# Conditioning product with w_cond as the moving operand, in two float32r parts

## The chip, the cores and the metric

The kernel runs on one core of a Trainium2 chip. The metric is the device time of one execution in microseconds (us). A core has five engines with a queue each: PE (matmul; its weight loads are shown apart as PEld), DVE (vector), ACT (scalar), POOL and SP. In this kernel SP issues most DMA transfers and POOL some.

## The reference

One layer of a decoder trunk on 2048 prompt rows and 64 sample rows (8 sequences of 8) of width 1024. Ahead of everything stands a conditioning by a vector c (one for the prompt, eight for the samples, so nine rows):

```python
def _layer(x, c, ...):
    mod = jax.nn.silu(c) @ w_cond + b_cond            # (9, 1024) @ (1024, 3072)
    shift, scale, gate = jnp.split(mod, 3, axis=-1)
    h = _rmsnorm(x, g_pre) * (1 + scale[:, None, :]) + shift[:, None, :]
    proj = h @ w_in                                    # (.., 1024) @ (1024, 10240)
    ...                                                # gMLP branch, dilated attention branch, merge
    out = merged @ w_out
    x_new = x + gate[:, None, :] * _rmsnorm(out, g_post)
```

The change touches the product for shift and scale alone, that is silu(c) times the first 2048 columns of w_cond, all in float32.

## The kernel before

The program is one stream of work without outer repetition. `conditioning` computes from c the two tables that everything else needs: `A` (1 + scale, times g_pre) and `Sh` (shift), each as 128 partitions x 8 blocks of 128 channels x 9 rows. Then the x tiles (16 of 128 prompt rows, one of 64 sample rows) are transposed on PE (L630), scaled and shifted by A and Sh (DVE L640, ACT L642) and split into two float16 parts hH and hL. From these the value projections of the first pattern are made (`v_tile`, L652 and after), and then, over some 2400 us, the query, key, value, gate and branch products, the attention, and the output projections.

A scheduler orders the instructions of each engine from the dependences and priorities; conditioning, the first units of w_in and the first x tile have high priority. Each queue runs in the order that the scheduler left. A tile from a pool with a number of buffers (`bufs`) waits, when the buffers are used up, until the readers of the oldest one are done.

Inside `conditioning`, in the order of the code:

- c9 (nine rows of c) is loaded, then w_cond in four chunks `wc` of 512 columns each (two loads of 1 MB per chunk, three buffers). Between the chunks the generator `loads_between` issues the load of x tile 0 (`x_tiles`, which also squares the tile on ACT, L712, takes the root, L167, and scales the tile, L715) and the first six loads of w_in (`wr`, L294).
- silu(c) is made from tanh (L202, L204, L205), transposed by eight small PE products (L208) and copied to `sc9`; scT holds it as two float32r parts (columns 0 to 8 the high part, 32 to 40 the rest), for later use in `gate_rows`.
- `vec` brings the small vectors, transposed at L214 into vecT.
- The product, L219 to L225: 16 blocks of 128 columns of w_cond, for each eight products with a 128x128 block of w_cond as the standing operand (the weights that PE loads first) and the nine columns of sc9 as the moving one. All 16 results stand in one PSUM bank, as columns of channels.
- L228 to L230 turn them into Sh and A. L232 to L248 find a scale `bm` over both and apply it.

Beside that, ACT takes absolute maxima of the w_in loads (L310, `junk`), from which their float16 scale comes.

`cond_mm` is a helper that `gate_rows` uses much later for the third part of w_cond: it splits a 128x512 tile into a high part wcH (ACT copy to float32r) and the rest wcL (DVE subtraction), and multiplies both with scT as the standing operand, so that rows 0 to 8 of the PSUM result belong to the high part of silu(c) and rows 32 to 40 to its rest.

Of the kernel before, what the change touches and what calls it, by code (L numbers as in the profile page):

```python
# [10 lines left out]
F32 = mybir.dt.float32  # L11
# [3 lines left out]
AF = mybir.ActivationFunctionType  # L15
ALU = mybir.AluOpType
AX = mybir.AxisListType

D = 1024
SEQ = 2048  # L20
KC = D // 128
# [48 lines left out]
def body(ctx, tc, I, O):  # L70
    nc = tc.nc
    PE, DMA = nc.tensor, nc.sync.dma_start

    V, S = nc.vector, nc.scalar
# [21 lines left out]
    CHB = 2  # L96
    WRB = 6
    HLB = 8
    BANKS = {"mm": 3, "s0": 1, "s1": 1, "o": 1, "t": 2}
    turn = [0]  # L100
    CXB = 3
# [5 lines left out]
    def bank(tag, shape=(128, 512), bufs=None, dt=F32):  # L107
        if tag == "s":
            turn[0] += 1
            tag = ("s0", "s1")[turn[0] % 2]  # L110
        return ps.tile(list(shape), dt, tag=tag, bufs=BANKS[tag], name=tag)

# [6 lines left out]
    ident = const.tile([128, 128], F32, name="ident")  # L119
# [30 lines left out]
    A = const.tile([128, KC, 9], F32, name="A")  # L150
# [10 lines left out]
    w_cond = I["w_cond"][0]  # L161
# [23 lines left out]
    def conditioning(cp, loads_between):  # L185
        c9 = cp.tile([9, D], F32, name="c9")
        DMA(c9[0:1], I["c_prompt"])
        DMA(c9[1:9], I["c_sample"])
        vec = cp.tile([40, 128], F32, name="vec")
        GDMA(vec[0:8], I["g_pre"].rearrange("o (k p) -> (o k) p", p=128))  # L190
        GDMA(vec[8:16], I["ln_v_g"].rearrange("o (k p) -> (o k) p", p=128))
        GDMA(vec[16:24], I["ln_v_b"].rearrange("o (k p) -> (o k) p", p=128))
        GDMA(vec[24:40], I["b_cond"][:, 0:2 * D].rearrange("o (k p) -> (o k) p", p=128))
        chunks = []
        for q in range(4):
            w = cp.tile([128, KC, 512], F32, tag="wc", bufs=3, name="wc")
            for k in (0, 4):
                DMA(w[:, k:k + 4], w_cond[k * 128:(k + 4) * 128, q * 512:(q + 1) * 512].rearrange("(k p) c -> p k c", p=128))
            chunks.append(w)
            loads_between(q)  # L200
        th = cp.tile([128, D], F32, tag="sq", bufs=1, name="th")[0:9]
        S.activation(th, c9, AF.Tanh, scale=0.5)  # L202
        V.memset(scT.bitcast(F32), 0.0)
        V.scalar_tensor_tensor(c9, th, 1.0, c9, op0=ALU.add, op1=ALU.mult)  # L204
        V.tensor_scalar(c9, c9, 0.5, None, op0=ALU.mult)  # L205
        pt = bank("t")
        for kc in range(KC):
            PE.transpose(pt[:, kc * 9:kc * 9 + 9], c9[:, kc * 128:(kc + 1) * 128], ident[0:9, 0:9])  # L208
        sc9 = cp.tile([128, KC, 9], F32, name="sc9")
        V.tensor_copy(sc9, pt[:, 0:72].rearrange("p (k n) -> p k n", n=9))  # L210
        S.activation(scT[:, :, 0:9], sc9, AF.Copy)
        V.tensor_tensor(scT[:, :, 32:41], sc9, scT[:, :, 0:9], op=ALU.subtract)
        pv = bank("t")
        PE.transpose(pv[:, 0:40], vec, ident[0:40, 0:40])  # L214
        vecT = cp.tile([128, 5, KC], F32, name="vecT")
        V.tensor_copy(vecT, pv[:, 0:40].rearrange("p (a k) -> p a k", a=5))
        V.tensor_copy(lngb, vecT[:, 1:3])

        pm = bank("o")  # L219
        for q in range(4):  # L220
            for j in range(4):
                o = (q * 4 + j) * 9
                for kc in range(KC):
                    PE.matmul(pm[:, o:o + 9], chunks[q][:, kc, j * 128:(j + 1) * 128], sc9[:, kc, :],  # L224
                              start=kc == 0, stop=kc == KC - 1)  # L225
        p4 = pm[:, 0:144].rearrange("p (a k n) -> p a k n", a=2, n=9)
        v4 = vecT.unsqueeze(3).to_broadcast([128, 5, KC, 9])
        V.tensor_tensor(Sh, p4[:, 0], v4[:, 3], op=ALU.add)  # L228
        V.scalar_tensor_tensor(A, p4[:, 1], 1.0, v4[:, 4], op0=ALU.add, op1=ALU.add)
        V.tensor_tensor(A, A, v4[:, 0], op=ALU.mult)  # L230

        bm = cp.tile([128, 2], F32, name="bm")  # L232
        for i, x in enumerate((A, Sh)):
            V.tensor_reduce(bm[:, i:i + 1], x.rearrange("p k n -> p (k n)"), axis=AX.X, op=ALU.max,
                            apply_absolute_value=True)
        V.tensor_tensor(bm[:, 0:1], bm[:, 0:1], bm[:, 1:2], op=ALU.add)
        pt = bank("t")
        PE.transpose(pt[0:1, 0:128], bm[:, 0:1], ident)
        b1 = cp.tile([1, 1], F32, name="b1")
        V.tensor_reduce(b1, pt[0:1, 0:128], axis=AX.X, op=ALU.max)  # L240
        pt = bank("t")
        PE.matmul(pt[:, 0:1], onesk[0:1, :], b1, start=True, stop=True)
        V.tensor_scalar(bm[:, 0:1], pt[:, 0:1], 32.0, 1e-30, op0=ALU.mult, op1=ALU.max)
        V.reciprocal(bm[:, 1:2], bm[:, 0:1])
        for x in (A, Sh):
            V.tensor_scalar(x, x, bm[:, 1:2], None, op0=ALU.mult)
        for i, f in enumerate((1.0, 0.5, -0.125)):
            V.tensor_scalar(hsc[:, i:i + 1], bm[:, 0:1], f, None, op0=ALU.mult)  # L248
# [454 lines left out]
    with tc.tile_pool(name="prep", bufs=1) as pp:  # L703
        loaded = {}

        def x_tiles():
            for i, (t0, n) in enumerate(tiles):
                xt = pp.tile([128, D], F32, tag="x", bufs=6, name="x")
                DMA(xt[0:n], x_src(i)[0])
                sq = pp.tile([128, D], F32, tag="sq", bufs=1, name="sq")  # L710
                r = rst[0:n, i:i + 1]
                S.activation(sq[0:n], xt[0:n], AF.Square, accum_out=r)  # L712
                rsqrt(r, n)
                eng = V if i % 2 or i == 0 else nc.gpsimd
                eng.tensor_scalar(xt[0:n], xt[0:n], r, None, op0=ALU.mult)  # L715
                loaded[i] = (t0, n, xt)
                yield

        xg = x_tiles()

        def loads_between(q):
            if q == 1:
                next(xg)
            if q == 2:
                next(loading)

        with tc.high_priority():
            conditioning(pp, loads_between)
            v0 = [load_unit16(OVV)]
            modulate(pp, [loaded[0]])  # L730
        v0.append(load_unit16(OVV + 512))
        DMA(masks, I["c_masks"])
        for batch in ((0,), (1,), (2, 3), (4, 5, 6, 7), (8, 9, 10, 11), (12, 13, 14, 15), (16,)):
            while batch[-1] not in loaded:
                next(xg)
            if batch[0]:
                modulate(pp, [loaded[i] for i in batch])
            for i in batch:
                for g in range(2):
                    v_tile(g, 0, *v0[g], *tiles[i])  # L740
                next(splitting)
# [592 lines left out]
```

## Time and profile before

| | |
|---|---|
| median of three runs | 2623.76 us (2620.62 to 2625.17) |
| profiled execution, its own time | 2629.5 us |
| its span, first to last instruction | 2627.7 us |
| busy: PE, PEld, DVE, ACT, POOL | 2509.3, 1817.9, 1589.1, 1110.8, 340.4 us |
| moved by DMA | 384.22 MB, mean 146 GB/s |

All lines of the profile are of one execution. Starts are us from the begin of the span. A line of a group gives the code line, the engine, the operation, output<-input by the program's tile names, count, busy time and mean ns of one; behind the bar what the engine waited for ahead of it. A line of a list of one tile gives the least, median and largest duration in ns. PE's matmul records overlap, so the distance between starts, not the duration, is what one costs in a stream.

### The profile page before, as it was taken

What the parts mean: (1) busy time and instruction counts of PE and PEld (TensorE: products, weight loads), DVE (VectorE), ACT (ScalarE), POOL (GpSimd) and SP (SyncE); (2) the same over time, 40 slices, a digit from 0 to 9 for tenths busy, and PEclk for the clock granted to TensorE, in tenths of its full rate; (3) what the DMA queues carried; (4) which work ended last, traced back from release to release, by engine and by line L of the source; (5) the groups of instructions that cost most, each with busy time, mean ns of one, the idle gap of its engine ahead of it and who ended that gap; (6) DMA issues with size and microseconds to landing.
All of it is one profiled execution on the core that took longest, in us unless ns stands there. A gap on an engine that the chain in (4) does not pass through costs nothing.

```text
span 2627.7 us, 48620 instructions
## 1 busy us (share of the span) xinstructions
PE 2509.3 (95%) x18678; PEld 1817.9 (69%) x18678; DVE 1589.1 (60%) x3590; ACT 1110.8 (42%) x2759; POOL 340.4 (13%) x459
## 2 busy tenths in 40 slices
PE   6899999999999989999989988999999999999998
PEld 6785768767677555555555677856556568898998
DVE  1663445878967789687877666854323235555553
ACT  2544556545545554544445423332323224343422
POOL 1020000120121211212012210001000001111110
PEclk9999999999999999999999999999999999999999
DMA  5323555576874777866687764352212057657552
GB/s 204 108 86 75 134 127 132 120 178 156 196 191 119 160 175 186 180 141 173 154 195 171 184 171 143 118 166 70 77 58 66 21 181 228 194 170 220 180 166 73
DMA packets 529863, 384.22 MB, mean 146 GB/s; under 512 B 184959, under 2 KB 472847, under 8 KB 529630
## 3 DMA queue, kind: packets, MB, share of 16 engines
q1 hardware_dynamic: 505022, 315.48, 44.7%
q0 software_dynamic: 24608, 65.63, 9.6%
q8 instruction: 146, 2.39, 0.4%
q14 instruction: 87, 0.71, 0.1%
HBM read 250.85 MB, written 90.78 MB: 130 GB/s over the span
## 4 chain that ended last, share of the span: by engine, by line
PE 69%; DMA 13%; DVE 9%; issue 6%; ACT 2%; SPq 1%; POOL 1%; DVEq 0%; ACTq 0%; POOLq 0%
PE mm L373 13%; PE mm L374 13%; PE mm L375 13%; PE mm L383 5%; PE mm L384 5%; PE mm L385 5%; DMA ch<-in_cache_kv_w 3%; PE o L224 2%; DMA wg<-in_w_cond 1%; PE s L892 1%; PE o L941 1%; DMA raw<-ya 1%; PE s L1153 1%; PE s L383 1%; DVE S L503 1%
## 5 line engine op out<-in xcount | busy, mean ns | idle before, releaser
L373 PE MATMUL mm<-hH,hl 128*128 128x512 f16 (+2 forms) x2240 | 770.7, 344 | 0.0
L374 PE MATMUL mm<-hL,hl 128*128 128x512 f16 (+2 forms) x2240 | 769.9, 344 | 0.0
L375 PE MATMUL mm<-hH,hl 128*128 128x512 f16 (+2 forms) x2240 | 769.6, 344 | 0.0
L383 PE MATMUL mm<-hl,hH 128*128 128x256 f16 x1536 | 418.4, 275 | 5.0 <-ACT zb L680 3.1
L384 PE MATMUL mm<-hl,hL 128*128 128x256 f16 x1536 | 420.7, 275 | 0.1
L385 PE MATMUL mm<-hl,hH 128*128 128x256 f16 x1536 | 420.3, 275 | 0.5 <-DVE hl L326 0.5
L373 PEld LDWEIGHTS <-hl 128*128 128x128 f16 x2240 | 223.3, 100 | 184.3 <-issue 10.1
L375 PEld LDWEIGHTS <-hl 128*128 128x128 f16 x2240 | 220.8, 99 | 181.4 <-issue 1.1
L374 PEld LDWEIGHTS <-hl 128*128 128x128 f16 x2240 | 220.6, 98 | 171.3 <-issue 0.6
L902 ACT ACTIVATE p<-p,sg 128x256 f32<-128x256 f32 (+1 forms) x384 | 172.4, 450 | 138.9 <-DVE sg L900 122.2
L430 POOL DMA_DIRECT2D ch<-in_cache_kv_w x104 | 93.2, 897 | 681.5 <-DVE pr L564 213.9
L383 PEld LDWEIGHTS <-hH 128*128 128x128 f16 x1536 | 152.3, 99 | 25.9 <-issue 4.8
L384 PEld LDWEIGHTS <-hL 128*128 128x128 f16 x1536 | 151.6, 99 | 25.2 <-issue 5.9
L385 PEld LDWEIGHTS <-hH 128*128 128x128 f16 x1536 | 151.8, 99 | 19.6 <-issue 1.2
L279 POOL TENSOR_TENSOR wl<-wr,wh 128x512 fp32r<-128x512 f32 x48 | 63.6, 1325 | 721.0 <-DMA wr<-in_w_proj_a 340.1
L278 ACT ACTIVATE wh<-wr 128x512 fp32r<-128x512 f32 x160 | 99.7, 630 | 124.6 <-PE mm L374 78.7
L900 DVE CUSTOM_DVE_ANT_0 p<-s,masks,cqk 128x256 f32<-128x256 f32 (+1 forms) x384 | 140.7, 419 | 16.9 <-PE s L892 16.8
L1186 ACT ACTIVATE e<-mm,scw 128x512 f32<-128x512 f32 (+2 forms) x40 | 24.5, 613 | 268.3 <-PE mm L375 268.3
L920 DVE SCALAR_TENSOR_TENSOR hl<-p,hl 128x1024 f16<-128x1024 f32 (+2 forms) x100 | 95.2, 953 | 59.9 <-ACT hl L919 59.6
L325 ACT ACTIVATE hl<-wr,scw 128x512 f16<-128x512 f32 x160 | 107.0, 712 | 51.1 <-DVE scw L317 38.3
L326 DVE SCALAR_TENSOR_TENSOR hl<-wr,scw,hl 128x512 f16<-128x512 f32 x160 | 115.6, 749 | 17.2 <-ACT hl L325 16.8
L373 PE MATMUL mm<-yaH,wh 128*128 128x512 f32 (+1 forms) x320 | 113.6, 355 | 2.6 <-DVE gts L1268 2.6
(426 smaller groups left out, 4644.0 us busy)
## 6 DMA issues: line engine op xcount, KB each, us to landing
ch<-in_cache_kv_w POOLq DMA_DIRECT2D x104, 512.0 KB, 6.1
wr<-in_w_in SPq DMA_DIRECT2D x160, 256.0 KB
wr<-in_w_proj_a SPq DMA_DIRECT2D x64, 256.0 KB
wr<-in_w_out SPq DMA_DIRECT2D x64, 256.0 KB
a<-sg SPq DMA_DIRECT2D x48, 264.0 KB
c<-a SPq DMA_DIRECT2D x48, 264.0 KB
v<-vt SPq DMA_DIRECT2D x96, 128.0 KB
vr<-v SPq DMA_DIRECT2D x48, 256.0 KB
```

The lines of the kernel that those rows point to most:

```text
L278: S.activation(H, raw, AF.Copy)
L325: S.activation(HL[:, 0], raw, AF.Copy, scale=sc[:, 0:1])
L326: V.scalar_tensor_tensor(HL[:, 1], raw, sc[:, 0:1], HL[:, 0], op0=ALU.mult, op1=ALU.subtract)
L373: PE.matmul(pt, h, xh[:, t0:t0 + n], start=kc == 0, stop=False)
L374: PE.matmul(pt, h, xl[:, t0:t0 + n], start=False, stop=False)
L375: PE.matmul(pt, l, xh[:, t0:t0 + n], start=False, stop=kc == m - 1)
L383: PE.matmul(pt, xh[:, t0:t0 + n], h, start=kc == 0, stop=False)
L384: PE.matmul(pt, xl[:, t0:t0 + n], h, start=False, stop=False)
L385: PE.matmul(pt, xh[:, t0:t0 + n], l, start=False, stop=kc == m - 1)
L900: V.tensor_tensor_reduce(x, sb[e][:, j, 0:nk], masks[:, 256 - nk:256], scale=cqk[:, i:i + 1], scalar=3e38, op0=ALU.add, op1=ALU.min, accum ...
L902: S.activation(x, x, AF.Exp, bias=mc, scale=-1.0, accum_out=lc)
L920: V.scalar_tensor_tensor(ll, x2, PSCALE, hh, op0=ALU.mult, op1=ALU.subtract)
```

## The change

w_cond becomes the moving operand. It is loaded in 16 tiles of 128x1024 (eight buffers): f = 0 holds the channels 0 to 511 of shift and of scale, f = 1 the channels 512 to 1023. Each tile is two 128x512 pieces, and `cond_mm` splits and multiplies each, now with three buffers for wcH and for wcL. The results are 41x512 in PSUM (two banks per half). They are copied to SBUF (`mod`), and four products per copy with 128 columns of `mod` standing and the constant `two` (two stacked identities) moving transpose them and add the two parts of silu(c) at once. A and Sh are then made by halves. sc9 is gone; scT is read from PSUM directly.

```diff
+    WCB = 8
...
+        chunks = [[], []]
+        for f in range(2):
+            for kc in range(KC):
+                w = cp.tile([128, D], F32, tag="wc", bufs=WCB, name="wc")
+                DMA(w.rearrange("p (a c) -> p a c", a=2),
+                    w_cond[kc * 128:(kc + 1) * 128, 0:2 * D].rearrange("p (a c) -> p a c", a=2)
+                    [:, :, f * 512:f * 512 + 512])
+                chunks[f].append(w)
+            loads_between(f)
...
-        chunks = []
-        for q in range(4):
-            w = cp.tile([128, KC, 512], F32, tag="wc", bufs=3, name="wc")
-            for k in (0, 4):
-                DMA(w[:, k:k + 4], w_cond[k * 128:(k + 4) * 128, q * 512:(q + 1) * 512].rearrange("(k p) c -> p k c", p=128))
-            chunks.append(w)
-            loads_between(q)
...
+        two = cp.tile([41, 9], F32, name="two")
+        V.memset(two, 0.0)
+        V.tensor_copy(two[0:9], ident[0:9, 0:9])
+        V.tensor_copy(two[32:41], ident[32:41, 32:41])
...
-        sc9 = cp.tile([128, KC, 9], F32, name="sc9")
-        V.tensor_copy(sc9, pt[:, 0:72].rearrange("p (k n) -> p k n", n=9))
-        S.activation(scT[:, :, 0:9], sc9, AF.Copy)
-        V.tensor_tensor(scT[:, :, 32:41], sc9, scT[:, :, 0:9], op=ALU.subtract)
+        p3 = pt[:, 0:72].rearrange("p (k n) -> p k n", n=9)
+        S.activation(scT[:, :, 0:9], p3, AF.Copy)
+        V.tensor_tensor(scT[:, :, 32:41], p3, scT[:, :, 0:9], op=ALU.subtract)
...
-        pm = bank("o")
-        for q in range(4):
-            for j in range(4):
-                o = (q * 4 + j) * 9
-                for kc in range(KC):
-                    PE.matmul(pm[:, o:o + 9], chunks[q][:, kc, j * 128:(j + 1) * 128], sc9[:, kc, :],
-                              start=kc == 0, stop=kc == KC - 1)
-        p4 = pm[:, 0:144].rearrange("p (a k n) -> p a k n", a=2, n=9)
-        v4 = vecT.unsqueeze(3).to_broadcast([128, 5, KC, 9])
-        V.tensor_tensor(Sh, p4[:, 0], v4[:, 3], op=ALU.add)
...
+        for f in range(2):
+            ks = slice(f * 4, f * 4 + 4)
+            pm = [bank(("mm", "s")[f]) for _ in range(2)]
+            for kc in range(KC):
+                cond_mm(cp, pm, kc, chunks[f][kc], D, 3)
+            pt = bank("t")
+            for n in range(2):
+                mod = cp.tile([41, 512], F32, tag="mod", bufs=4, name="mod")
+                if n % 2:
+                    S.activation(mod, pm[n][0:41, :], AF.Copy)
+                else:
+                    V.tensor_copy(mod, pm[n][0:41, :])
+                for j in range(4):
+                    PE.matmul(pt[:, (4 * n + j) * 9:(4 * n + j) * 9 + 9], mod[:, j * 128:(j + 1) * 128], two,
+                              start=True, stop=True)
+            p4 = pt[:, 0:72].rearrange("p (a k n) -> p a k n", a=2, n=9)
+            v4 = vecT[:, :, ks].unsqueeze(3).to_broadcast([128, 5, 4, 9])
+            V.tensor_tensor(Sh[:, ks], p4[:, 0], v4[:, 3], op=ALU.add)
...
         def loads_between(q):
-            if q == 1:
-                next(xg)
-            if q == 2:
-                next(loading)
+            next((xg, loading)[q])
```

What this does to the order of the engines, first on ACT from the transpose of silu(c) on, before the change (line numbers are those of the listing):

```order
L211 ACTIVATE scT<-sc_186 128x8x9
L310 ACTIVATE junk,mx<-wr 128x512 x4
L712 ACTIVATE sq,rst<-x 128x1024
L167 ACT_TABLE_LOAD
L167 ACTIVATE rst<-rst 128x1
L712 ACTIVATE sq,rst<-x 128x1024
```

The rows go on with three more pairs of square and root and then with the first hH of the x tiles. The same place after the change, where line numbers are up to 14 higher (L181 is the copy in `cond_mm`, L726 the square, L168 the root, L324 the maximum):

```order
L181 ACTIVATE wcH<-wc 128x512 x3
L726 ACTIVATE sq,rst<-x 128x1024
L168 ACT_TABLE_LOAD
L168 ACTIVATE rst<-rst 128x1
L205 ACT_TABLE_LOAD
L205 ACTIVATE th<-c_133 9x1024
L217 ACTIVATE scT<-t 128x8x9
L181 ACTIVATE wcH<-wc 128x512 x2
L726 ACTIVATE sq,rst<-x 128x1024
L181 ACTIVATE wcH<-wc 128x512
L168 ACT_TABLE_LOAD
L168 ACTIVATE rst<-rst 128x1
```

Three copies moved ahead of the first square and the tanh, and the other 29 stand among the squares, roots and maxima.

On PE the place of the product, before:

```order
L630 MATMUL s_379<-ident,x 128x128
L630 MATMUL s_391<-ident,x 128x128
L208 MATMUL t<-ident,c_133 128x9 x8
L214 MATMUL t<-ident,vec 128x40
L224 MATMUL o<-sc_186,wc 128x9 x128
L238 MATMUL t<-ident,bm 1x128
```

and the end of the product after the change (L183 and L184 multiply wcH and wcL, L238 transposes `mod`, L644 an x tile):

```order
L183 MATMUL s_331<-wcH,scT 41x512
L183 MATMUL s_332<-wcH,scT 41x512
L184 MATMUL s_331<-wcL,scT 41x512
L184 MATMUL s_332<-wcL,scT 41x512
L238 MATMUL t<-two,mod 128x9 x4
L644 MATMUL s_497<-ident,x 128x128
L238 MATMUL t<-two,mod 128x9 x4
L644 MATMUL s_509<-ident,x 128x128
L252 MATMUL t<-ident,bm 1x128
```

The 128 products (two records each in the profile) became 64, and the first two transposes of x moved from ahead of them to behind them.

On SP the start of the loads, before:

```order
L198 DMA wc<-in_w_cond 128x4x512 x4
L709 DMA x<-in_x_prompt 128x1024
L198 DMA wc<-in_w_cond 128x4x512 x2
L294 DMA wr<-in_w_in 128x2x256 x6
L732 DMA masks<-in_c_masks 128x256
L709 DMA x<-in_x_prompt 128x1024 x5
L198 DMA wc<-in_w_cond 128x4x512 x2
```

and after:

```order
L194 DMA wc<-in_w_cond 128x2x512 x7
L723 DMA x<-in_x_prompt 128x1024
L194 DMA wc<-in_w_cond 128x2x512
L308 DMA wr<-in_w_in 128x2x256 x6
L743 DMA masks<-in_c_masks 128x256
L723 DMA x<-in_x_prompt 128x1024 x5
L194 DMA wc<-in_w_cond 128x2x512 x7
```

One load of wc stands ahead of these rows, before `ident`. The last seven wait for buffers of the first half, as the last two did for the first chunk.

More of the change, by code (lines that the diff above doesn't have):

```diff
@@ L217, in conditioning @@
         V.tensor_copy(lngb, vecT[:, 1:3])
-        pm = bank("o")
-        for q in range(4):
-            for j in range(4):
-                o = (q * 4 + j) * 9
-                for kc in range(KC):
-                    PE.matmul(pm[:, o:o + 9], chunks[q][:, kc, j * 128:(j + 1) * 128], sc9[:, kc, :],
-                              start=kc == 0, stop=kc == KC - 1)
-        p4 = pm[:, 0:144].rearrange("p (a k n) -> p a k n", a=2, n=9)
-        v4 = vecT.unsqueeze(3).to_broadcast([128, 5, KC, 9])
-        V.tensor_tensor(Sh, p4[:, 0], v4[:, 3], op=ALU.add)
-        V.scalar_tensor_tensor(A, p4[:, 1], 1.0, v4[:, 4], op0=ALU.add, op1=ALU.add)
-        V.tensor_tensor(A, A, v4[:, 0], op=ALU.mult)
+        for f in range(2):
[16 more added lines that the diff above has]
+            V.tensor_tensor(Sh[:, ks], p4[:, 0], v4[:, 3], op=ALU.add)
+            V.scalar_tensor_tensor(A[:, ks], p4[:, 1], 1.0, v4[:, 4], op0=ALU.add, op1=ALU.add)
+            V.tensor_tensor(A[:, ks], A[:, ks], v4[:, 0], op=ALU.mult)
         bm = cp.tile([128, 2], F32, name="bm")
```

## The prediction

> **What bounds the kernel now.** I read the page first (busy shares, chain), then stretches of the span, then the start instruction by instruction.
>
> ```profile
> PE 2509.3 (95%) x18678; PEld 1817.9 (69%) x18678; DVE 1589.1 (60%) x3590; ACT 1110.8 (42%) x2759; POOL 340.4 (13%) x459
> ...
> 0.00:25.17 25.17, 1.96 (x11) 1.38 (x11) 3.72 (x10) 6.37 (x8) 2.44 (x8) 1.00 0.93 329
> 25.17:80.00 54.83, 54.79 (x256) 54.69 (x256) 3.72 (x13) 11.09 (x25) 5.76 (x2) 1.00 0.25 93
> 80.00:100.00 20.00, 13.30 (x58) 8.86 (x59) 16.16 (x54) 14.26 (x35) 2.85 (x1) 0.92 0.30 90
> 100.00:200.00 100.00, 96.89 (x866) 85.16 (x864) 64.35 (x156) 52.72 (x115) 17.78 (x10) 1.00 0.36 119
> ```
>
> Columns of the stretches: length, then busy time (and count) of PE, PEld, DVE, ACT and POOL, granted clock, DMA share, GB/s. PE is the bound of the whole kernel at 95%, but that average hides the start: from 25.17 to 80.00 us PE does one thing only, while DVE works 3.7 us, ACT 11.1 us and the DMA is idle three quarters of the time. The chain of waits names it:
>
> ```profile
> 21.85 1.22 DVE c L204
> 23.10 0.69 DVE c L205
> 23.83 1.03 PE t L208 x8
> 24.88 0.24 DVE sc L210
> 25.17 54.80 PE o L224 x256
> 80.00 0.23 DVE Sh L228
> ```
>
> ```profile
> L224 PEld LDWEIGHTS o<-sc,wc x256: 288/333/338, 25.2 to 79.5; 128*128 128x128 f32 x128
> L224 PE MATMUL o<-sc,wc x256: 362/362/383, 25.2 to 79.6; 128*128 128x9 f32 x128
> ```
>
> The conditioning product stands alone on the chain: 54.80 / 256 = 0.214 us for a record that streams 9 columns but first loads 128x128 of w_cond, and the loads are busy without a gap. Nothing else can start: DVE's first use of the result (Sh, L228) is at 80.00. A shorter product therefore moves everything behind it.
>
> **The change part by part.** *Removed:* the 256 records, 54.8 us of chain. *Added:* w_cond is cut into 32 tiles of 128x512; each gets an ACT copy to float32r, a DVE subtraction and two PE products with scT (41 columns) standing and 512 columns moving. The same helper already runs in gate_rows:
>
> ```profile
> L180 ACT ACTIVATE wcH<-wg x16: 620/629/630, 1495.6 to 1604.1; 128x512 fp32r<-128x512 f32 x16
> L181 DVE TENSOR_TENSOR wcL<-wg,wcH x16: 673/693/693, 1496.3 to 1605.0; 128x512 fp32r<-128x512 f32 x16
> L182 PE MATMUL o<-wcH,scT x16: 422/428/648, 1496.3 to 1604.8; 128*41 128x512 f32 x16
> 2164.15 1.24 ACT L278 ACTIVATE wh<-wr 128x512 fp32r<-128x512 f32 x2 [0.55 <-DMA wr<-in_w_proj_a]
> 2204.31 0.40 PE L373 MATMUL mm<-ybH,wh 128*128 128x512 f32 x1
> 2204.54 0.40 PE L374 MATMUL mm<-ybL,wh 128*128 128x512 f32 x1
> ```
>
> So a copy costs 0.62 us in a row of copies (1.24 for two), a subtraction 0.69, a product 0.43 alone and 0.23 in a stream (2204.31 to 2204.54). Per engine: ACT 32 x 0.62 = 19.8 us, DVE 32 x 0.69 = 22.1, PE 64 x 0.23 = 14.7. Beside these, ACT has work of its own in that stretch, which lay hidden under the 54.8 us and now does not:
>
> ```profile
> 25.32 0.61 ACT L310 ACTIVATE junk<-wr 128x512 f16<-128x512 f32 x1
> ...
> 28.31 1.06 ACT L712 ACTIVATE sq<-x 128x1024 f32<-128x1024 f32 x1
> ...
> 29.47 1.28 ACT L167 ACT_TABLE_LOAD   x1
> ...
> 32.34 1.04 ACT L712 ACTIVATE sq<-x 128x1024 f32<-128x1024 f32 x1
> ...
> 33.70 1.04 ACT L712 ACTIVATE sq<-x 128x1024 f32<-128x1024 f32 x1
> ```
>
> Four L310 maxima take 28.31 - 25.32 = 3.0 us, one x tile's square with its root 33.70 - 32.34 = 1.36, a table 1.28. DVE's other work there, 3.7 us in the stretch above, leaves DVE at some 26 us, behind ACT. The order after the change puts all of ACT's extra work between the copies, so ACT is the new bound, and I sum along it.
>
> *Start.* It stays where the tanh puts it:
>
> ```profile
> 16.70 1.06 ACT L712 ACTIVATE sq<-x 128x1024 f32<-128x1024 f32 x1 [14.69 <-DMA x<-in_x_prompt]
> ...
> 20.76 1.05 ACT L202 ACTIVATE th<-c 9x1024 f32<-9x1024 f32 x1
> ```
>
> ACT waits 14.69 us for the first x tile; ahead of it on SP's queue stand 4.2 MB of w_cond, before and after. The three copies that now stand ahead of that square fit into the wait, and no more than three, because wcH has three buffers until PE may consume. Now both halves of scT must be there first; they are read from PSUM directly (the copy of 0.24 at 24.88 goes), but the low half comes behind vecT:
>
> ```profile
> L211 ACT ACTIVATE scT<-sc 128x72 fp32r<-128x72 f32 x1 | 0.3, 266 | 3.3 <-DVE sc L210 3.3
> ...
> L212 DVE TENSOR_TENSOR scT<-sc,scT 128x72 fp32r<-128x72 f32 x1 | 0.2, 228 | 0.0
> L216 DVE COPY vecT<-t 128x40 f32<-128x40 f32 x1 | 0.2, 200 | 0.0
> ```
>
> High half 24.9 to 25.15, vecT to 25.35, low half to 25.6: first product 25.65. ACT's fourth copy needs the first product's end: 25.65 + 0.43 = 26.1.
>
> *ACT from 26.1 to its last copy:* 29 copies x 0.62 = 18.0; five x tiles x 1.36 = 6.8; table 1.3; four maxima 3.0; the first half's PSUM copy 0.6. Sum 29.7: last copy ends at 55.8.
>
> *Tail.* Subtraction 0.7, product 0.45, PSUM copy 0.6, then eight small products with mod standing plus one x transpose, 9 x 0.21 + 0.15 = 2.0 (these have no row; nearest is L224, 0.214 each, below that the gaps between transposes at 88 us, also 0.21): 3.8 us. Sh starts at 59.6 instead of 80.00, which is 20.4 us less. The PSUM copy is priced by its nearest row:
>
> ```profile
> L775 ACT ACTIVATE qh<-mm x60: 361/580/598, 208.9 to 1320.1; 128x512 f16<-128x512 f32 x36, 128x256 f16<-128x256 f32 x24
> ```
>
> The waits between three engines, some 0.03 us each, and DVE falling behind in runs of five copies (0.69 against 0.62) have no row; nothing to 3 us, and I take 0.9. Gain 19.5 us.
>
> *Moved: loads.* The 8.4 MB of w_cond now come as 16 loads of 0.5 MB in the same 2 KB rows. SP issues eight, x tile 0, one more, the first six w_in loads, masks, five x tiles, then seven that each wait for a buffer of the first half. SP is not blocked early: the ninth needs only the first buffer, read by the early copies.
>
> ```profile
> 5.00:10.00 5.00, 0.00 (x0) 0.00 (x0) 0.00 (x0) 0.00 (x0) 0.00 (x0) 1.00 1.05 395
> ...
> 40.00:45.00 5.00, 5.00 (x25) 5.00 (x25) 0.00 (x0) 0.00 (x0) 0.00 (x0) 1.00 0.99 337
> 45.00:50.00 5.00, 5.00 (x25) 5.00 (x25) 0.00 (x0) 0.00 (x0) 0.00 (x0) 1.00 0.22 82
> ```
>
> At 390 GB/s the 9.6 MB ahead of the last seven are in by about 29 us. Of the seven, the first is released near 27 us, the last when ACT and DVE have read the eighth tile pair, near 42. Before, the last 2 MB were issued at 39.03 (quoted below) and were in by about 46, 7 us for four times as much; so the last lands before 49, and its copies come near 54. Cost nothing; the cover is 5 us. Behind the seven on SP stand the seventh w_in load and x tile 6, which wait for later buffers anyway (x tile 6 went out at 89.57).
>
> ```profile
> 39.03 0.93 SPq L198 DMA_DIRECT2D wc<-in_w_cond  x2
> ...
> 89.57 4.59 DMA x<-in_x_prompt
> ```
>
> *Carried to the end?* Two x transposes that ran at 20.5 us now stand at the tail, 0.2 us of it counted above. Behind Sh the chain is the same, and from the end of the v tiles on the orders of ACT, DVE, SP and POOL agree row for row. PE is busy 96.89 of 100 us from 100 to 200, and nothing there has a fixed time. Up to 3 us either way may come from the changed mix of ACT and DVE around the first v tiles.
>
> *A rule against this change.* At 88 to 92 us PE's 256-column products start 0.21 us apart and later half that, and after an idle gap the record shows the half clock:
>
> ```profile
> 92.10 0.42 PE L383 MATMUL mm<-hl,hH 128*128 128x256 f16 x1
> 92.32 0.42 PE L384 MATMUL mm<-hl,hL 128*128 128x256 f16 x1
> 93.54 0.27 PE L385 MATMUL mm<-hl,hH 128*128 128x256 f16 x1
> 93.65 0.27 PE L630 MATMUL s<-ident,x 128*128 128x128 f32 x1
> 97.00:98.00 1.00, 1.00 (x6) 0.68 (x5) 1.00 (x1) 1.00 (x3) 1.00 (x1) 0.50 0.01 2
> ```
>
> A PE that waits for tiles may thus run its 512-column products 0.43 us apart: 64 x 0.43 = 27.5 us, still under ACT's 29.7, but over it in the last 14 tiles (12.0 against 14 x 0.62 + 3.0 = 11.7). The Trainium skill, "TensorE: Matmul & The Clock Gate", section "What's actually happening", says just this, that the clock halves after an idle window of about 3.4 us and returns after as long a busy one. By the half rate throughout the sum would lose 1 to 2 us, by the full rate nothing.
>
> **The rivals.** *Coarser overlap (0.13).* In-order queues with three buffers, PE at half clock, POOL's two 2.9 us operations on x beside DVE's subtractions: if a tile costs 1.35 us instead of 29.7 / 29 = 1.02, 29 x 0.33 = 9.6 us of the gain go and the time is 2614. For it: PE, DVE and ACT wait on each other in every tile. Against: at full clock no engine but ACT has more than 26 us of work in these 30.
> *Not carried (0.07).* The v tiles wait for x loads (4.59 us at 89.57); were they paced by these, the gain would vanish there: 2622. Against: x tile 6 is issued when tile 0's buffer comes free, so it moves along.
> *One engine at a time (0.04, slower).* If each tile went through copy, subtraction and product in turn, it would cost 0.66 + 0.72 + 0.45 = 1.83 us; 29 x 1.83 = 53.1, Sh at 26.1 + 53.1 + 3.8 = 83.0: 3 us slower, 2627. It decides above (80.0 - 29.9) / 29 = 1.73 us a tile. In gate_rows, which has one buffer, the engines do take turns; here three buffers and the order, with three copies ahead of the first product, speak against it.
> *Four passes (0.01, slower).* A product of four passes would give 64 x 4 x 0.23 = 58.9 us and Sh near 88; time 2632. The 0.43 of L182, the same shape and type, excludes it nearly. The Trainium skill, "FP8 and Floating Point Precision", section "TensorE Precision Notes", gives true FP32 four passes; no run here shows float32r taking them.
>
> **How the numbers follow.** The sum was made on an execution of 2629.5 us (span 2627.7, 1.8 around it), 5.7 above the median 2623.8 of the runs, of which it takes the same piece: 2623.8 - 19.5 = 2604.3, I say 2604. The forecast, a gain of 15 to 25 us (2599 to 2609), has 0.75. Its ends: were DVE's 26 us the bound instead of ACT's 29.7, it would be 3.7 more; waits of 3 us and half clock give 4 less; the carry adds 3 either way. The runs themselves spread over 4.6 us. For 8 in 10, with the better half of the coarse case, I take 2597 to 2614. A change of 0.2%, 5.2 us, is about what can be told from none. Faster: 0.75 and the coarse case 0.13, 0.88; same 0.07; slower 0.05.
>
> **What would show it.** Right: Sh near 60 us; ACT nearly gapless from 26 to 56, DVE and PE with gaps; no wait for wc loads after 27 us; the later stretches shifted by the same amount. Wrong: ACT idle on PE's wcH buffers, copies waiting for wc loads, Sh after 65, or a stretch beyond 100 us that takes longer than before.

## The result and the profile after

The changed kernel took 2603.18 us (median; 2596.12 to 2606.97) against 2624.15 us for the kernel before beside it (2620.62 to 2625.17): ratio 0.9919, 95% interval 0.9896 to 0.9943, 21 us less. In two later sets, which come below, the same pair gave 14.0 and 13.0 us. The forecast was 2604, a gain of 15 to 25 us.

The profiled execution took 2603.74 us, 0.6 above the median. First its page and four stretches (length; busy time and count of PE, PEld, DVE, ACT, POOL; granted clock; DMA share; GB/s), to be laid beside those of the kernel before:

```profile
span 2601.9 us, 48441 instructions
...
PE 2479.4 (95%) x18518; PEld 1771.1 (68%) x18518; DVE 1608.6 (62%) x3629; ACT 1129.5 (43%) x2793; POOL 340.3 (13%) x459
...
25.70:59.00 33.30, 28.64 (x89) 13.01 (x89) 23.83 (x47) 26.64 (x56) 6.05 (x2) 0.80 0.48 155
45.00:54.00 9.00, 9.00 (x26) 4.62 (x25) 6.64 (x15) 6.38 (x14) 0.02 (x1) 0.50 0.18 57
61.40:191.70 130.30, 116.48 (x972) 97.05 (x973) 82.15 (x220) 71.66 (x159) 20.93 (x11) 0.96 0.35 113
191.70:2601.90 2410.20, 2331.96 (x17441) 1658.89 (x17439) 1496.94 (x3349) 1022.59 (x2568) 310.86 (x438) 0.99 0.56 148
```

The stretch in which PE worked alone for 54.8 us has become one of 33 us in which PE, ACT and DVE are all busy. The last two rows are the v tiles (from Sh to the first query product) and all that follows. The same two of the kernel before:

```profile
80.00:208.90 128.90, 119.09 (x975) 99.14 (x976) 84.03 (x220) 71.06 (x159) 20.63 (x11) 0.99 0.35 114
208.90:2627.70 2418.80, 2333.45 (x17438) 1662.72 (x17436) 1497.65 (x3349) 1022.25 (x2569) 311.62 (x438) 0.99 0.56 147
```

Of the 25.8 us between the two spans, 18.6 lie ahead of Sh, the v tiles give 1.4 back, and 8.6 come from the 2400 us behind, which the change does not touch. Whether those belong to it is the first thing to settle.

The chain of the start in the changed kernel (start, length, engine, tile and line; L181 is the copy, L182 the subtraction, L183 and L184 the products, L238 the small transposing products):

```profile
27.60 0.66 PE mm L183
...
42.34 0.53 ACT wcH L181
42.91 0.42 PE mm L183
43.34 0.99 PE t L238 x8
...
47.15 1.80 PE t L238 x8
...
53.05 0.70 DVE wcL L182
53.78 0.48 ACT wcH L181
...
59.09 1.06 PE t L238 x8
```

From the first product to 42.9 the chain goes through ACT and DVE, from 42.9 to 53 through PE alone, and then through ACT and DVE again. The middle piece is the one that the granted clock of 0.50 shows above: the products of that stretch start 0.43 us apart, and a group of eight small records takes 1.80 us where the groups at 43.34 and 59.09 take 0.99 and 1.06. This is one execution; the repeats below differ in this piece.

ACT's own rows (last bracket: idle time ahead, and what ended it):

```profile
18.76 1.06 ACT L726 ACTIVATE sq<-x 128x1024 f32<-128x1024 f32 x1 [8.79 <-DMA x<-in_x_prompt]
...
28.29 0.63 ACT L181 ACTIVATE wcH<-wc 128x512 fp32r<-128x512 f32 x1 [1.10 <-PE mm L183]
...
32.84 1.04 ACT L726 ACTIVATE sq<-x 128x1024 f32<-128x1024 f32 x1
...
34.92 0.28 ACT L168 ACTIVATE rst<-rst 128x1 f32<-128x1 f32 x1
35.11 0.61 ACT L181 ACTIVATE wcH<-wc 128x512 fp32r<-128x512 f32 x1
...
36.67 1.66 ACT L181 ACTIVATE wcH<-wc 128x512 fp32r<-128x512 f32 x3
38.24 0.28 ACT L168 ACTIVATE rst<-rst 128x1 f32<-128x1 f32 x1
...
49.99 0.63 ACT L181 ACTIVATE wcH<-wc 128x512 fp32r<-128x512 f32 x1 [2.18 <-PE s L183]
...
56.47 1.14 ACT L181 ACTIVATE wcH<-wc 128x512 fp32r<-128x512 f32 x2
```

The last copy ends at 57.6, and DVE adds the vector at 61.43:

```profile
61.43 0.20 DVE L242 TENSOR_TENSOR Sh<-t,vecT 128x36 f32<-128x36 f32 x1 [2.40 <-PE t L238]
```

### The profile page after: what moved, and what is told of

It reads as the page before. It is cut to its first block, busy times and chain, and to the rows that moved or that the text cites. A ratio compares the mean times of both kernels' runs of the same rounds, so it can differ in the third digit from the quotient of the medians.

```text
span 2601.9 us, 48441 instructions
## 1 busy us (share of the span) xinstructions
PE 2479.4 (95%) x18518; PEld 1771.1 (68%) x18518; DVE 1608.6 (62%) x3629; ACT 1129.5 (43%) x2793; POOL 340.3 (13%) x459
## 4 chain that ended last, share of the span: by engine, by line
PE 62%; DMA 14%; DVE 12%; issue 7%; ACT 4%; POOL 1%; SPq 1%; DVEq 0%; ACTq 0%; POOLq 0%
PE mm L387 13%; PE mm L388 12%; PE mm L389 12%; PE mm L397 4%; PE mm L398 4%; PE mm L399 4%; DMA ch<-in_cache_kv_w 3%; DVE S L517 1%; PE s L1164 1%; DVE acc L583 1%; PE s L903 1%; PE s L397 1%; DMA raw<-ya 1%; PE o L398 1%; PE o L397 1%
## 5 line engine op out<-in xcount | busy, mean ns | idle before, releaser
L397 PE MATMUL mm<-hl,hH 128*128 128x256 f16 x1536 | 416.5, 274 | 10.8 <-ACT vt L666 4.2
L397 PEld LDWEIGHTS <-hH 128*128 128x128 f16 x1536 | 151.7, 99 | 26.7 <-issue 5.4
```

Of the source, the lines that this page charges most:

```text
L397: PE.matmul(pt, xh[:, t0:t0 + n], h, start=kc == 0, stop=False)
```

## The experiments

Three theories stood at the beginning. *Overlap*: the product runs at ACT's rate behind a start that the tanh sets, and its gain goes through to the end. *PE rate*: the gain comes from PE's part alone, that is from w_cond moving instead of standing, and the split matters little. *Engine turns*: what decides is whether the three engines work at once. The kernels below were timed in three sets, each on one chip with the kernel before beside it (medians of before: 2618.77, 2618.22, 2618.98). Ratios are to that kernel. The changed kernel itself is not in the first of these sets (early tanh, float32 without parts, no low part, copy twice), so its Sh is taken from its own traces.

### Start or rate: the tanh first

The tanh and the two DVE operations on c9 are written ahead of the loads, so that x tile 0 no longer stands ahead of them on ACT.

```diff
...
+        th = cp.tile([128, D], F32, tag="sq", bufs=1, name="th")[0:9]
+        S.activation(th, c9, AF.Tanh, scale=0.5)
+        V.scalar_tensor_tensor(c9, th, 1.0, c9, op0=ALU.add, op1=ALU.mult)
+        V.tensor_scalar(c9, c9, 0.5, None, op0=ALU.mult)
         chunks = [[], []]
...
```

> tanh of c and the two operations behind it are written ahead of the loads, so ACT does them before the first x tile's square and not after it. In the changed kernel the first product stands at 27.6 us, of which the wait for x tile 0 (until 18.8) and two tables are most. Theory 'the start is a term of its own': c9 is in by about 4 us, scT by about 9, the products then follow the loads; ACT's 29 us of work and PE's start from 9 instead of 28. Sh should begin at 43 to 46 us instead of 61.4, and the time fall by about 16 us, to about 2587. Rival 'only ACT's idle time counts': ACT was idle for some 12 us before 28, and its later work also waits for x tiles and w_in loads that come no earlier: Sh at 49 to 52, time about 2592. Rival 'the gain is not carried': Sh early, time 2600 or more.

Measured: 2594.93 us, ratio 0.9905 (0.9884 to 0.9927). From its trace, ACT, PE and DVE:

```profile
4.35 1.05 ACT L191 ACTIVATE th<-c 9x1024 f32<-9x1024 f32 x1
9.36 0.65 PE L183 MATMUL mm<-wcH,scT 128*41 128x512 f32 x1 [0.93 <-DVE scT L218]
46.16 0.20 DVE L242 TENSOR_TENSOR Sh<-t,vecT 128x36 f32<-128x36 f32 x1 [2.39 <-PE t L238]
```

The tanh moved up by 18.5 us, the first product by 18.2 and Sh by 15.3. So the wait for x tile 0 through the tanh did set the start. The stretch behind it, from the first product to Sh, is 3 us longer (36.8 against 33.8, or 32.4 and 32.3 in the repeats); one row of the waits from 9 to 47 us (total, times, longest) that the changed kernel does not have there explains 1.7 us of that, a copy that now waits for its load; what makes up the rest was not tried:

```profile
ACT wcH L181 <- DMA wc<-in_w_cond: 1.7, 1, 1.7
```

Sh comes just behind the 43 to 46 us of the first theory. The time does not fall by the 16 us that it gave: beside the changed kernel it is 9.9 and 7.3 us less in the sets below.

### Moving operand or split: float32 without parts

w_cond moves unsplit in float32 against the nine columns of sc9; there are 32 products, and no copies or subtractions of w_cond. The results and the copies `mod` have nine rows.

```diff
-                cond_mm(cp, pm, kc, chunks[f][kc], D, 3)
+                for n in range(2):
+                    PE.matmul(pm[n][0:9, :], sc9[:, kc, :], chunks[f][kc][:, n * 512:(n + 1) * 512],
+                              start=kc == 0, stop=kc == KC - 1)
...
```

> The operands stay turned (w_cond moves), but w_cond is not split: one float32 product of 9 standing and 512 moving columns per piece, 32 in all, no copy on ACT and no subtraction on DVE. Theory 'it is the turning that pays, if a float32 product of 512 columns takes four times the 0.23 us of a float32r one': 32 x 0.92 = 29.4 us from 27.2 on plus a tail of 3.1, Sh at 60, time as the changed kernel (2603). If it takes one pass: 7 us, the loads of the second half become the end, Sh near 42, time about 2585. If PE stays at half clock with four passes: 32 x 1.7 = 55 us, Sh near 85, time near before (2627): then the split is what pays.

Measured: 2608.23 us, ratio 0.9958 (0.9945 to 0.9971). PE's rows of the first half, as a list of one tile (least, median, largest ns) and in the timeline, and DVE's end:

```profile
L227 PE MATMUL mm<-wc,sc x32: 592/592/1061, 27.9 to 43.3; 128*9 128x512 f32 x32
27.88 16.03 PE L227 MATMUL mm<-wc,sc 128*9 128x512 f32 x32
61.88 0.20 DVE L241 TENSOR_TENSOR Sh<-t,vecT 128x36 f32<-128x36 f32 x1 [2.41 <-PE t L237]
```

Sixteen products show 32 records in 16.03 us: 1.00 us for a float32 product of 512 columns, about four times the 0.23 to 0.25 us of a float32r one. Without splitting on ACT and DVE, Sh comes at 61.88; in the three traces of the split version it comes at 61.4, 59.1 and 59.4. From the first product to Sh it takes 34.0 us, the split version 33.8, 32.4 and 32.3. Turning the operands is thus what pays for nearly all of the gain at Sh: 256 records of 0.214 us became 64 of 0.50. The split saves PE time, but the work of ACT and DVE that it needs uses up all of that saving but 0.2 to 1.7 us. In time this kernel gains 10.5 us on the kernel before, the split version 13.0 to 21.0 in other sets; what the split is worth in time, side by side, no run shows.

### ACT or PE: no low part, and the copy twice

In the first kernel the low part of w_cond is left out of this product: 32 products and no subtraction, with ACT's copies as they were. In the second ACT makes each high part twice.

```diff
             S.activation(H, x, AF.Copy)
+            PE.matmul(pm[n][0:41, :], scT[:, kc, :], H, start=kc == 0, stop=not low and kc == KC - 1)
+            if not low:
+                continue
...
-                cond_mm(cp, pm, kc, chunks[f][kc], D, 3)
+                cond_mm(cp, pm, kc, chunks[f][kc], D, 3, False)
```

> Leaves out the low part of w_cond: no subtraction on DVE and no second product, 32 products instead of 64; ACT's copies stay. Theory 'ACT is the bound' (the prediction's sum): Sh moves only by the waits between the engines and by the shorter tail, to 57 to 59 us from 61.4. Rival 'PE at half clock is the bound in the second half' (its products stand 0.43 us apart from 45 to 54 us): 32 products less are up to 32 x 0.43 = 14 us less, Sh near 48 to 50. Time 2600 against 2591.

```diff
             S.activation(H, x, AF.Copy)
+            if twice:
+                S.activation(H, x, AF.Copy)
...
-                cond_mm(cp, pm, kc, chunks[f][kc], D, 3)
+                cond_mm(cp, pm, kc, chunks[f][kc], D, 3, True)
```

> ACT makes each high part twice (32 more copies of 0.53 us, and one more table load). Theory 'ACT is the bound': 29 copies x 0.53 + 1.3 = 16.7 us more on the chain, Sh at 78, time about 2620. Rival 'PE and DVE set the pace': ACT had 33.3 - 26.6 = 6.7 us free between 25.7 and 59, which the copies fill first: Sh near 71, time about 2613.

Measured: 2600.77 us (ratio 0.9929, 0.9904 to 0.9955) and 2625.64 us (1.0024, 1.0002 to 1.0047). First product and Sh of the kernel without low part, then of the one with two copies:

```profile
26.08 3.06 PE L181 MATMUL mm<-wcH,scT 128*41 128x512 f32 x6 [0.43 <-DVE scT L220]
58.72 0.20 DVE L244 TENSOR_TENSOR Sh<-t,vecT 128x36 f32<-128x36 f32 x1 [4.46 <-PE t L240]
```

```profile
27.22 0.65 PE L185 MATMUL mm<-wcH,scT 128*41 128x512 f32 x1 [0.43 <-DVE scT L220]
74.29 0.20 DVE L244 TENSOR_TENSOR Sh<-t,vecT 128x36 f32<-128x36 f32 x1 [4.68 <-PE t L240]
```

With half of PE's products and all of DVE's subtractions gone, the stretch from first product to Sh is 32.6 us instead of 33.8, and the repeats of the changed kernel have 32.4 and 32.3: what PE and DVE do for the low part costs nothing that could be told from one execution to the next. In the other kernel 29 of the 32 more copies stand behind the first product (three are made ahead of it), at 0.52 us each 15.1 us. The stretch is 47.1 us: 13.3 more than in the first trace of the changed kernel, where ACT waited 2.8 us for PE behind its fourth copy, and 14.7 more than in the repeats, where no such wait is longer than 0.23 us. Both runs say that ACT sets the rate. Sh at 74.3 lies between the 78 and the 71 us that had been expected, and the time is 5.6 us above the higher of the two.

The second kernel shows one thing more. Its Sh is 5.7 us earlier than before, and yet it measures slower, if by little. Its v tiles:

```profile
74.30:214.80 140.50, 122.64 (x973) 100.50 (x974) 82.78 (x220) 71.44 (x160) 20.89 (x11) 0.91 0.32 104
```

They take 140.5 us, 12 more than before, at a granted clock of 0.91 against 0.99. ACT waits 10.0 us for x tiles there, against 6.0 before; this one trace was not followed further. An earlier Sh is thus not always carried whole; we come back to it.

### Overlap or not: one buffer

wcH and wcL get one buffer instead of three, so that copy, subtraction and product of a tile must follow one another.

```diff
-                cond_mm(cp, pm, kc, chunks[f][kc], D, 3)
+                cond_mm(cp, pm, kc, chunks[f][kc], D, 1)
```

> wcH and wcL have one buffer each instead of three, so that ACT may not run ahead. The prediction's rival of one engine at a time: 1.83 us a tile, Sh at about 88 us, slower than before by some 8 us. If only the buffers bind (a copy waits for the subtraction of the tile before it, 0.63 + 0.03 + 0.69 = 1.35 us a tile, while product and copy overlap): 31 x 1.38 = 43 us from 28, Sh near 75, a gain over the kernel before of about 5 us left. Theory that the buffers do not matter: Sh as in the changed kernel, 61.

Measured: 2636.86 us, ratio 1.0073 (1.0045 to 1.01): slower than before. Its ACT copies wait for DVE, and Sh comes late:

```profile
60.53 0.63 ACT L181 ACTIVATE wcH<-wc 128x512 fp32r<-128x512 f32 x1 [2.09 <-DVE wcL L182]
86.69 0.20 DVE L242 TENSOR_TENSOR Sh<-t,vecT 128x36 f32<-128x36 f32 x1 [4.75 <-PE t L238]
```

The first product stands at 27.06; less the tail of 3.8, 55.8 us go to 31 tiles, 1.80 each. That is the price of the rival in which one engine works at a time (1.83), on the wrong side of its 1.73. The time is 18.6 us above the kernel before, in two runs, where the expectation had some 8. The three buffers make the difference between a gain and a loss. So all three theories hold in part: the turned operand brings the gain at Sh, ACT's rate sets the length of the split product, and without overlap the gain is lost.

### The late start: larger loads

w_cond comes in loads of 1 MB as before the change (four 128x4x512 tiles for each half, four buffers), ahead of x tile 0 the same bytes as in the changed kernel.

```diff
...
-                w = cp.tile([128, D], F32, tag="wc", bufs=WCB, name="wc")
...
+                    w = cp.tile([128, 4, 512], F32, tag="wc", bufs=WCB // 2, name="wc")
+                    DMA(w, w_cond[k * 128:(k + 4) * 128, q * D + f * 512:q * D + f * 512 + 512].rearrange("(k p) c -> p k c", p=128))
...
```

> The first half and the second half of w_cond come in four loads of 1 MB each, as in the kernel before, instead of eight of 0.5 MB; the product is the changed one. The prediction put the start 2.0 us too early, because x tile 0 was in at 18.8 us and not at 16.7. Theory 'the size of the loads': x tile 0 in at 16.7, the first product at 25.6, Sh at 59.5. Rival 'it varies from one execution to the next' (17.2, 18.4 and 18.8 in three other kernels with the small loads): in at 17 to 19, Sh at 60 to 62.

Measured: 2604.94 us, ratio 0.9952 (0.993 to 0.9974), no different from the unedited change beside it (2604.21). But its start is the predicted one:

```profile
16.52 1.06 ACT L727 ACTIVATE sq<-x 128x1024 f32<-128x1024 f32 x1 [5.60 <-DMA x<-in_x_prompt]
25.36 0.65 PE L183 MATMUL mm<-wcH,scT 128*41 128x512 f32 x1 [0.43 <-DVE scT L219]
```

x tile 0 is there at 16.52 instead of 18.76, the first product comes at 25.36 instead of 27.60, and Sh at 57.8 instead of 61.4 (59.1 and 59.4 in the repeats). In the seven traces of kernels with the small loads and the tanh behind x tile 0, that tile came at 17.2 to 18.8. The rate of the DMA from 5 to 10 us tells a part of why, first with 1 MB loads, then in the changed kernel:

```profile
5.00:10.00 5.00, 0.00 (x0) 0.00 (x0) 1.02 (x3) 0.85 (x2) 0.00 (x0) 1.00 1.05 389
```

```profile
5.00:10.00 5.00, 0.00 (x0) 0.00 (x0) 1.62 (x4) 1.78 (x3) 0.00 (x0) 1.00 0.96 309
```

389 against 309 GB/s, 0.4 MB in 5 us, which is 1 us of the 2.2 at 390 GB/s. The rest goes with what moved beside x tile 0: when it was in, 5.15 MB had moved with the larger loads (and 5.14 in the kernel before), 5.65 with the smaller ones, so half a megabyte from behind it on the queue came in ahead of its end. Why the smaller loads start slower and let more past was not tried.

### What the end of the run shows: repeats

To learn whether the 8.6 us behind the v tiles belong to the change, the three kernels of interest ran again unedited: the changed one, the one with the early tanh, and the one before.

> The changed kernel once more, unedited, on the same chip as the next one, since the kernel with the early tanh stood 15.3 us ahead of it at Sh and yet was, on another chip and against the kernel before there, only some 3 us faster (23.8 against 21.0 us gained). Theory 'part of a head start is lost in the v tiles': its gain over the kernel before is 18 to 23 us here too, and the early tanh's only 3 to 8 us more. Rival 'chips differ': on one chip the early tanh is 11 to 15 us faster than this one, which then gains 9 to 13 us over the kernel before.

> The kernel with the early tanh, unedited, beside the changed kernel. Sh at 46 us again. Its v tiles took 134.6 us from Sh to the first qh against 130.3 in the changed kernel, with a granted clock of 0.94 against 0.96. Theory 'part of a head start is lost in the v tiles': about 10.9 us ahead at the first qh, and 8 to 11 us faster at the end. Rival 'not carried': within 5 us of the changed kernel.

> The kernel before, unedited, against itself. The changed kernel had Sh 18.6 us earlier on one chip and 20.9 on another and gained 21 us by the median there, 14 here. Theory 'the stretch from the first qh to the end varies by some 10 us from one execution to the next, in every kernel' (2410 and 2420 us in two executions of the changed kernel, 2416 and 2408 in two of the early tanh): the ratio to itself is 1 within 0.2%, Sh at 79 to 81, 129 us from there to the first qh, and then 2407 to 2420 us to the end. Rival 'the changed kernel's order costs some 6 us behind the first qh': here always 2411 us or less.

> The kernel before once more, for a second profile on this chip: Sh at 79 to 81, the first qh 129 us later; from there to the end 2407 to 2420 us by the theory of varying executions, 2411 or less by its rival.

> The changed kernel a third time, beside the kernel before on one more stretch of runs: Sh at 59 to 62 us, the first qh 129 to 131 us later, a gain of 14 to 21 us by the median. By the theory of varying executions the mean gain over all chips comes to that at the first qh, 17 to 20 us; by the rival it stays at 14.

> The early tanh a third time beside the changed kernel: Sh at 46 to 47, 10 to 12 us faster than the changed kernel.

Measured, with Sh, the stretch of the v tiles and all that follows from each trace (us; the third repeat of before was profiled only):

| kernel | time | ratio, 95% interval | Sh | v tiles | the rest | span |
|---|---|---|---|---|---|---|
| before | 2624.15 | 1 | 80.0 | 128.9 | 2418.8 | 2627.7 |
| before, again | 2619.36 | 0.9997 (0.9979 to 1.0014) | 80.2 | 128.2 | 2413.8 | 2622.2 |
| before, third | | | 79.9 | 128.4 | 2412.3 | 2620.6 |
| changed | 2603.18 | 0.9919 (0.9896 to 0.9943) | 61.4 | 130.3 | 2410.2 | 2601.9 |
| changed, again | 2604.21 | 0.9949 (0.9932 to 0.9966) | 59.1 | 129.7 | 2420.4 | 2609.2 |
| changed, third | 2606.01 | 0.9952 (0.9937 to 0.9967) | 59.4 | 131.7 | 2413.9 | 2605.0 |
| early tanh | 2594.93 | 0.9905 (0.9884 to 0.9927) | 46.2 | 134.6 | 2416.0 | 2596.8 |
| early tanh, again | 2594.27 | 0.9905 (0.9888 to 0.9922) | 47.1 | 131.3 | 2407.6 | 2586.0 |
| early tanh, third | 2598.68 | 0.9916 (0.9897 to 0.9935) | 46.2 | 132.3 | 2417.1 | 2595.6 |

The rows of the windows from which the extremes of "the rest" come, the changed kernel again and before for the third time:

```profile
188.80:2609.20 2420.40, 2338.13 (x17441) 1662.89 (x17439) 1496.62 (x3349) 1022.66 (x2568) 310.69 (x438) 0.99 0.56 147
```

```profile
208.30:2620.60 2412.30, 2332.75 (x17439) 1660.89 (x17437) 1496.88 (x3349) 1022.84 (x2569) 311.94 (x438) 0.99 0.56 148
```

The rest takes 2412 to 2419 us before the change and 2410 to 2420 after it, with means of 2415.0 and 2414.8. In three traces it varies by 6.5 us in the kernel before, 10.2 in the changed one and 9.5 with the early tanh. The 8.6 us in the first pair of traces are thus within what two executions differ by, and no sign of the change; three traces each do not exclude an effect of a few us.

What remains is the lead at the first query product: mean 208.5 before, 190.5 after, 18.0 us. It was 20.1 at Sh; the v tiles give 2.1 back. The medians of the three pairs give 21.0, 14.0 and 13.0 us, mean 16. The profiled executions of before took 2629.5, 2624.0 and 2622.4 us, on average 4.5 above the medians beside them, those of the changed kernel 2.7 above: that is most of the 2 us between the two means. That the later two medians lie 4 to 5 us under the lead stays open; their 95% intervals reach from 8.6 to 17.8 us. The expected 17 to 20 us did not come, and both sets are nearer to the 14 of the rival, by which the new order costs something late, though that rival's sign, a rest of 2411 us or less before the change, did not show in any trace.

The early tanh was faster than the change on both chips where both ran, by 9.9 us (8 to 11 expected) and 7.3 us (10 to 12 expected), and beats both kernels: about 23 us under the kernel before. Of the 13 us by which its Sh leads, about two more go in the v tiles. What PE waits for there is seen in the waits over just this stretch (total, times, longest), first before, then the changed kernel, then the early tanh (first):

```profile
PE mm L383 <- ACT hl L325: 0.5, 1, 0.5
```

```profile
PE mm L397 <- ACT vt L666: 2.0, 2, 1.7
PE mm L397 <- ACT hl L339: 2.0, 1, 2.0
```

```profile
PE mm L397 <- ACT vt L666: 4.0, 3, 2.2
PE mm L397 <- ACT hl L339: 3.3, 1, 3.3
```

L383 is L397 after the change, and before it PE had no wait for vt at all. So PE waits 3.5 us longer for ACT's vt and hl in the changed kernel and 6.8 longer with the early tanh, where the stretch gives back 1.4 and 5.7. The two waits return in every repeat (together 4.9 and 4.2 us in the changed kernel, 6.6 and 6.4 with the early tanh, 0.3 and 0.5 before), but the length of the stretch does not follow them one to one: with 6.6 it is 131.3 us, with 4.2 it is 131.7. It is not the x tiles: ACT's waits for them over the stretch went from 6.0 to 4.4 and 4.8 us. Nor need it be the lead: with one buffer Sh comes later than before the change, and the stretch still takes 132.7 us (86.7 to 219.4). That speaks for the new order of the instructions. Why ACT itself is late there was not tried.

## Why the prediction was right, step by step

**Start: mis-sized by 2.0 us.** The prediction let the first product stand "where the tanh puts it", at 25.65; it came at 27.60 (26.65 and 27.12 in the repeats). The tanh did set it, as its move by 18 us shows, but x tile 0, behind which the tanh waits, was in at 18.76 instead of 16.70 (17.81 and 18.28 in the repeats). The step that failed is the one that passed from "4.2 MB ahead of it, before and after" to the same time: equal bytes in half-size loads came at 309 GB/s from 5 to 10 us instead of 395, and 0.5 MB more had moved when x tile 0 was in. Larger loads gave the predicted start back.

**ACT's sum: 29.7 predicted, 29.3 measured in the first trace** (28.29 to 57.6) **and 26.9 in both repeats**: its terms were too large. A copy in a row of copies costs 0.52 us, not 0.62: three of them go from 36.67 to 38.24, where the root behind them starts. The price of 0.62 was half of a record of two, and a record is longer than the distance to the next start (one of 0.61 at 35.11 is followed at 35.63). An x tile costs 1.04 + 0.19 = 1.23 (32.84 to 33.88, 34.92 to 35.11), not 1.36; a maximum 0.62, not 0.75. So ACT's own work is some 26 us, and most of the other 3 in the first trace are waits for PE, of which 2.18 us stand in one place, ahead of the copy at 49.99. There PE had the small products of the first half in its queue, 1.80 us at half clock (47.15 in the chain), ahead of the products that free wcH. The prediction counted those on ACT's side as a PSUM copy, but not on PE's. In both repeats the granted clock was 1.00 from 45 to 54 us and that wait is missing. ACT in the first repeat, whose fourth copy starts at 27.34:

```profile
46.09 2.04 ACT L181 ACTIVATE wcH<-wc 128x512 fp32r<-128x512 f32 x3 [0.18 <-issue]
...
53.09 1.14 ACT L181 ACTIVATE wcH<-wc 128x512 fp32r<-128x512 f32 x2
```

So the sum was 2.8 us too large, and in the first trace waits that it did not have made up for that.

**The rule against it was right in kind, in one of three executions.** In the first trace the products stand 0.43 us apart from 44.8 to 53.6, with a granted clock of 0.50, and the chain runs through PE there; in the repeats they do not. The prediction gave this case 1 to 2 us, while its own comparison (12.0 against 11.7) gives 0.3; with the measured prices ACT's side of the last 14 tiles is 14 x 0.52 + 4 x 0.62 = 9.8 us and the loss 2.2, near the 2.6 us in which ACT waited. The Trainium skill, "TensorE: Matmul & The Clock Gate", section "What's actually happening", knows only these two speeds, and the trace agrees; it lets the clock fall after an idle window of about 3.4 us, and that the trace does not show for the fall at 44.8, since PE was busy for 2.79 of the 3.40 us before it, and from 42.00 to 44.80 for 2.31 of 2.80 us:

```profile
42.00:44.80 2.80, 2.31 (x12) 1.46 (x13) 2.36 (x5) 2.69 (x8) 2.63 (x1) 0.97 0.81 282
```

**Tail: right in the first trace, 1 us short in the repeats.** 3.8 us predicted, 57.6 to 61.43 measured, and 4.9 and 4.7 in the repeats (54.2 to 59.1 and 54.7 to 59.4). The eight small products are 16 records, in two groups of 1.06 and 1.00 us: 0.26 us a product, where the prediction took 0.21. In the repeats the second group takes 1.87 us.

**Loads: right.** From 26 to 62 us no copy waits for w_cond; three of the longest waits of the product in that stretch (total, times, longest):

```profile
PEld mm L183 <- ACT wcH L181: 6.6, 11, 2.3
DVE wcL L182 <- ACT wcH L181: 4.1, 6, 1.3
...
ACT wcH L181 <- PE s L183: 2.6, 3, 2.2
```

PE and DVE wait for ACT, as the forecast wanted. "ACT nearly gapless" held but for those 2.6 us, and the sign that would have spoken against it, ACT idle on PE, appears at one place of any size and not in the repeats.

**Carry: right within its 3 us.** Sh was forecast at 59.6 and came at 61.4, 59.1 and 59.4. That is met within 2 us by terms that offset each other: in the repeats the fourth copy starts 1.2 and 1.7 us late, ACT's piece is 2.8 short and the tail 1.1 and 0.9 long. The 20 us at Sh are 18 at the first query product, and the stretch behind that is the same on average. The v tiles' 2 us lie within the carry of "up to 3 us either way", though not by the x loads that the rival named. Luck helped here: the first measurement's 21.0 us lies above the 19.5 forecast, and the other two, 14.0 and 13.0, lie below it and outside the 15 to 25. The changed kernel took 2603 to 2606 us in all three sets; the kernel before took 2624 in the first and 2618 to 2619 in the later ones, so that the gain came out so near owes much to the first set.

**The rivals.** One engine at a time: its mechanism and price were right (1.80 measured, 1.83 forecast), and so was the reason against it, the three buffers. Four passes: a float32 product costs 1.00 us, about four times a float32r one, so the float32r products did not pay that price. Not carried: true for a tenth of the lead. Coarser overlap: 29.3 and 26.9 us instead of 39.

## What to carry to other kernels

When a product is bound by loading weights for a few moving columns (0.214 us for nine), make the big operand the moving one first; splitting it to get a faster data type comes second (under 2 us of the start here) and pays only as far as the engines that split it have time and buffers (one buffer here turned 13 to 21 us of gain into 19 of loss). Then ask what now stands at the head: moving one tanh ahead of a wait for an unrelated tile was worth another 7 to 10 us. Price an operation in a row by the distance of starts, not by its record, and compare stretches, the early ones too, over several executions before giving a difference to a change or reading a bound from one trace.

## What the runs showed of the hardware that was not expected

- A float32 product with 512 moving columns is two records of 0.50 us, 1.00 us in all, and one with 9 moving columns two records of 0.214 us; float32r with 512 columns takes 0.23 us at full clock and 0.43 at half. The first products after the start stood 0.43 us apart too, for 3.4 us in the first trace and 4.7 in the first repeat, while the granted clock was recorded as 1.00.
- Loads of 0.5 MB at the begin of the changed kernel moved 309 to 321 GB/s from 5 to 10 us, loads of 1 MB with the same 2 KB rows 389 to 396.
- The granted clock fell to 0.50 while PE had waits of no more than 0.43 us in the 2.8 us before. In the two repeats of the same kernel it stayed at 1.00 there. Behind PE's longest wait in the product it fell too where that was 2.0 us (first trace and second repeat) and not where it was 1.6 (first repeat).
- The same 17440 PE records behind the v tiles took 2408 to 2420 us in nine traces, with the same granted clock of 0.99 in all of them.
